# SwiGLU of a hybrid encoder block on one core: ten gate/up pairs become five token-major quads

## The chip, the core and the metric

The kernel runs on one core of a Trainium2 chip. The metric is the device time of one launch in microseconds (us), and of several runs the median. Five engines work side by side, each through its own list of instructions in order: TensorE (PE, with the loading of its stationary operand shown as PEld), VectorE (DVE), ScalarE (ACT), GpSimd (POOL) and SyncE (SP). In this kernel SP issues most transfers, POOL the others.

## The reference, cut to what matters

```python
x = x + merged @ w_o                 # two token mixers before this, unchanged here
h2 = rmsnorm(x, g_ffn)
x = x + (silu(h2 @ w_ff_gate) * (h2 @ w_ff_up)) @ w_ff_down
return rmsnorm(x, g_final)
```

There are 512 tokens, a model width of 1024 and a hidden width of 2816. All is float32. The change lies wholly in the third line.

## The kernel before, in words

Every operand x is split into a rounded part, hi, in the type fp32r and the remainder lo = x - hi (`split`, lines 200 to 210: ScalarE casts, VectorE subtracts). A product is three matmuls: hi hi, hi lo, lo hi. The large products go by the Strassen-Winograd scheme with seven products of quarters instead of eight. The forms of the activations are called a11, a12, a22, s1 to s4, those of the weights b11, b21, t1 to t4, b22.

`PLAN` lists the weight units in the order of use. `take` hands out the next unit and prepares two more: SP loads quarters into ten `raw` buffers, four entries of the plan earlier; VectorE adds quarters for the t forms (line 301); ScalarE and VectorE split the result into one of five buffers `whi` and `wlo`. For a few quads (`SUMMED`) the sums of quarters are made in DRAM by POOL's accumulating transfers, and VectorE adds nothing.

A Tile scheduler lays the instructions of every engine into a fixed order when the kernel is built; a wait is a semaphore. So the order on an engine is not that of the code, and an instruction that waits holds up all behind it on its engine.

SwiGLU runs like this. The hidden columns are 11 pairs of 256 gate and 256 up columns. A pair's quad is feature-major: the weight is the stationary operand, 256 tokens move past it, and the result has hidden features on the partitions and tokens along the free axis (`prod`, line 383; 24 matmuls of 256 columns per product). That is the layout that the down product needs for its stationary operand, so `gated` (lines 1125 to 1157) applies silu and the product and writes the seven activation forms straight from there. After 3, 7 and 11 pairs (`FF_PARTS`) comes a down product over the pairs since then, token-major (`prod_tm`, line 427; 512 columns per matmul, tokens on the partitions). The first two results go to DRAM through POOL (`put_first`, `add_y`), the last is joined with them and normalised.

`pair` (line 1173) holds the products of a pair; `beside` names products of later pairs that are put between, so that PE has something to do while a pair's activations are made.

Of the kernel before, what the change touches and what calls it, by code (L numbers as in the profile page):

```python
# [41 lines left out]
FF_PARTS = ((0, 3), (3, 4), (7, 4))  # L42
# [11 lines left out]
WIDTH = {"w": 512, "x": 256, "a": 512, "o": 512, "f": 256, "d": 512}  # L54
# [4 lines left out]


FIRST_PRODUCTS = ((0, "b11"), (0, "b21"), (1, "b11"), (1, "b21"), (2, "b11"), (2, "b21"))


def beside(q):

    if q < 5:
        return None, ((q + 6) // 2, "b21" if q % 2 else "b11")
    return (q, "b21"), (q + 1, "b11") if q + 1 < NQ else None


def plan():
# [42 lines left out]
    def f(q, *names):  # L114
        for n in names:
            out.append(("q", ("f", q), n, 0, 4))

    for q, name in FIRST_PRODUCTS:
        f(q, name)
    for q0, n in FF_PARTS:  # L120
        for q in range(q0, q0 + n):
            between, behind = beside(q)
            f(q, "t1", "t2")
            if between:
                f(*between)
            f(q, "t3")
            if behind:
                f(*behind)
            f(q, "t4", "b22")
        units = [(name, u) for name in FORMS for u in range(0, n, 2)]  # L130
        if q0 + n == NQ:

            i = units.index(("b21", 2))
            units[i:i + 3] = units[i + 1:i + 3] + units[i:i + 1]
        for name, u in units:
            out.append(("q", ("d", q0), name, u, min(2, n - u)))
    return out
# [9 lines left out]
SUMMED = (("f", 0), ("f", 1), ("o",))  # L147


def parts(quad):  # L150
    return (0, 2) if quad == ("o",) else (0,)


def loads():
# [3 lines left out]
    for i, x in enumerate(PLAN):  # L158
        if x[0] == "q":
            _, quad, name, u, nk = x  # L160
            need = name if quad in SUMMED else NEEDS.get(name)
            if need:
                out.append((i, quad, need, u, nk * WIDTH[quad[0]]))
# [4 lines left out]
QUARTERS = [x for x in LOADS if x[2][0] == "b"]  # L168
# [3 lines left out]
def block_kernel(ctx: ExitStack, tc: tile.TileContext, xw0, xw, xT, xtok, wpack, wquad, cols, decs, rot, g_ffn, g_final, out):  # L172
# [90 lines left out]
    steps = {"quads": sums_of(SUMMED[:2]), "heads": sums_of(SUMMED[2:])}  # L263
# [850 lines left out]
    gates = {}  # L1114

    q_add, gate_of = FF_PARTS[1][0], [None]

    def act_tiles(names):
        hi, lo = bigtile(F32R), bigtile(F32R)
        for j, n in enumerate(names):  # L1120
            act[n] = tuple(t[:, 2 * j:2 * j + 2, :].rearrange("p a (b c) -> p (a b) c", c=256) for t in (hi, lo))
        return hi.rearrange("p (f a) (b c) -> p f (a b) c", f=2, c=256), \
            lo.rearrange("p (f a) (b c) -> p f (a b) c", f=2, c=256)

    def gated(q, th, g, u):

        q0, _ = part_of[q]
        i = q - q0  # L1130
        if not gates.get(q0):
            t = bigtile(F32R)
            gates[q0] = [act_tiles(("a11", "a12")), act_tiles(("s1", "s3")), act_tiles(("s2", "s4"))]
            act["a22"] = tuple(t[:, 2 * j:2 * j + 2, :].rearrange("p a (b c) -> p (a b) c", c=256)
                               for j in range(2))
# [3 lines left out]
        nc.vector.tensor_tensor(out=s, in0=u, in1=s, op=ALU.mult)  # L1139

        def both(j, t):
            split(t.rearrange("p (s t) -> p s t", s=2), *(x[:, :, i, :] for x in gates[q0][j]))
        E, O = slice(0, 256), slice(256, 512)
        if th == 1:
            split(s[:, O], *(x[:, i, :] for x in act["a22"]))
        else:
            both(0, s)
        gates[q, th] = s
        if (q, 1 - th) not in gates:
            return  # L1150
        x1, x2 = gates.pop((q, 0)), gates.pop((q, 1))
        v, w = t512(), t512()
        for o, a, b, op in ((v[:, E], x2[:, E], x2[:, O], ALU.subtract), (v[:, O], x1[:, E], x2[:, E], ALU.subtract),
                            (w[:, E], v[:, E], x1[:, E], ALU.subtract), (w[:, O], x1[:, O], w[:, E], ALU.add)):
            nc.vector.tensor_tensor(out=o, in0=a, in1=b, op=op)
        both(1, v)
        both(2, w)
# [3 lines left out]
    def first_tokens(q, name):  # L1161

        _, (w,) = take()
        ps = bank()
        if name == "b11":
            prod(w, XF[0, 0], ps, True)
            heads_of[q] = {"a": ps, "p1": snap(ps)}
        else:
            prod(w, XF[1, 0], ps, True)
            g = heads_of[q]["p1"]  # L1170
            nc.vector.tensor_tensor(out=g, in0=ps, in1=g, op=ALU.add)

    def pair(q):
        st = heads_of[q]
        a, d = st["a"], bank()
        between, behind = beside(q)
        _, (w,) = take()
        if between:
            prod(w, XF["s1"], d, True)
            _, (w,) = take()  # L1180
            prod(w, XF["s2"], a, False)
            u2 = snap(a)
            first_tokens(*between)
        else:
            _, (w2,) = take()
            prod(w2, XF["s2"], a, False)
            u2 = snap(a)
            prod(w, XF["s1"], d, True)
# [235 lines left out]
```

## Time and profile before

| what | value |
|---|---|
| median of 3 runs | 1022.72 us (1022.34 to 1023.39) |
| profiled execution, first to last instruction | 1021.7 us |
| PE busy | 1013.2 us, 99% |
| VectorE busy | 902.5 us, 88% |
| ScalarE busy | 548.4 us, 54% |
| POOL busy | 151.7 us, 15% |
| moved by DMA | 202.34 MB, mean 198 GB/s |

The profile gives no time of its own for the profiled execution beside its span; the median of the runs is 1.0 us above the span. A row of a group reads: line, engine, operation, output and input tiles with shapes, count, then busy time, the mean of one in ns, and the idle time of the engine ahead of them with what ended it. A mean is the length of one instruction; where neighbours overlap, the engine's busy time is less than the sum of lengths. In the chain of waits the merged rows give start, length and the number of instructions.

### The profile page before, as it was taken

The numbers are of one execution on the slowest core, as the hardware profiler recorded it, in microseconds if no ns is written. First come the engines' busy times: TensorE is split into PE (matmuls) and PEld (weight loads), VectorE is DVE, ScalarE is ACT, GpSimd is POOL, SyncE is SP. The second block draws the span as 40 slices with busy tenths as digits, with TensorE's granted clock in tenths as the row PEclk, the third lists the DMA queues.
The fourth block names the chain that finished last, engine by engine and source line by source line (L and its number), as shares of the span: only waits on it lengthen the run. The fifth ranks groups of instructions, "written<-read, shape, count | busy, mean of one in ns | idle before, by whom it ended". The sixth has DMA issues, their size and how long they took to land.

```text
span 1021.7 us, 14821 instructions
## 1 busy us (share of the span) xinstructions
PE 1013.2 (99%) x5586; PEld 883.2 (86%) x5586; DVE 902.5 (88%) x1161; ACT 548.4 (54%) x744; POOL 151.7 (15%) x238
## 2 busy tenths in 40 slices
PE   9999999999999999999999999999999999999997
PEld 7888888888888998888888888889998999899986
DVE  7878998979798888797989997999898999889996
ACT  7547665553655455343543325586654565556554
POOL 0030221222122003202122100020001410110011
PEclk9999999999999999999999999999999999999999
DMA  9525587695767657839597855484316562663523
GB/s 354 188 81 185 173 296 212 214 310 162 249 196 238 250 203 268 333 130 349 124 331 294 272 200 169 157 264 132 107 42 242 172 154 83 198 153 104 165 69 98
DMA packets 53992, 202.34 MB, mean 198 GB/s; under 512 B 7392, under 2 KB 7520, under 8 KB 49312
## 3 DMA queue, kind: packets, MB, share of 16 engines
q1 hardware_dynamic: 37600, 137.39, 39.0%
q0 software_dynamic: 16032, 63.71, 21.3%
q8 instruction: 44, 0.72, 0.3%
q10 hardware_dynamic: 288, 0.29, 0.1%
q14 instruction: 28, 0.23, 0.1%
HBM read 162.82 MB, written 57.41 MB: 216 GB/s over the span
## 4 chain that ended last, share of the span: by engine, by line
PE 98%; DVE 1%; ACT 0%; issue 0%; POOL 0%; POOLq 0%; ACTq 0%
PE bank L427 39%; PE bank L383 27%; PE bank L342 10%; PE bank L343 10%; PE bank L344 10%; PE bank L477 0%; PE bank L1053 0%; PE bank L998 0%; PE bank L662 0%; DVE raw L301 0%; DVE big L1296 0%; ACT whi L203 0%; DVE wlo L204 0%; POOL fin L1286 0%; POOL ac L1035 0%
## 5 line engine op out<-in xcount | busy, mean ns | idle before, releaser
L203 ACT CAST whi<-raw 128x1024 fp32r<-128x1024 f32 (+2 forms) x299 | 302.8, 1028 | 265.0 <-PE bank L427 67.1
L204 DVE TENSOR_TENSOR wlo<-raw,whi 128x1024 fp32r<-128x1024 f32 (+2 forms) x300 | 352.7, 1192 | 68.0 <-ACT whi L203 67.7
L383 PE MATMUL bank<-xform,whi 128*128 128x256 f32 x1424 | 258.2, 284 | 0.3 <-ACT whi L203 0.3
L383 PEld LDWEIGHTS bank<-xform,whi 128*128 128x128 f32 x1424 | 222.3, 192 | 2.0 <-ACT t L434 0.8
L383 PE MATMUL bank<-xform,wlo 128*128 128x256 f32 x712 | 200.7, 283 | 0.0
L427 PE MATMUL bank<-whi,big 128*128 128x512 f32 x596 | 187.0, 389 | 0.0
L427 PE MATMUL bank<-whi,xform 128*128 128x512 f32 x496 | 157.1, 390 | 0.0
L301 DVE TENSOR_TENSOR raw<-raw 128x1024 f32<-128x1024 f32 (+1 forms) x128 | 152.0, 1203 | 4.2 <-DMA raw<-wquad 3.3
L383 PEld LDWEIGHTS bank<-xform,wlo 128*128 128x128 f32 x712 | 136.4, 192 | 0.0
L427 PEld LDWEIGHTS bank<-whi,big 128*128 128x128 f32 x596 | 111.9, 188 | 23.8 <-ACT t L434 0.4
L427 PE MATMUL bank<-wlo,big 128*128 128x512 f32 x298 | 115.7, 389 | 0.0
L427 PEld LDWEIGHTS bank<-whi,xform 128*128 128x128 f32 x496 | 93.0, 188 | 19.7 <-DVE xform L204 0.6
L427 PE MATMUL bank<-wlo,xform 128*128 128x512 f32 x248 | 96.5, 389 | 0.0
L434 ACT COPY t<-bank 128x512 f32<-128x512 f32 x105 | 61.0, 587 | 56.3 <-PE bank L383 30.1
L342 PE MATMUL bank<-big,whi 128*128 128x512 f32 x220 | 85.7, 390 | 0.0
L344 PE MATMUL bank<-big,wlo 128*128 128x512 f32 x220 | 85.6, 389 | 0.0
L343 PE MATMUL bank<-big,whi 128*128 128x512 f32 x220 | 85.6, 389 | 0.0
L427 PEld LDWEIGHTS bank<-wlo,big 128*128 128x128 f32 x298 | 56.0, 188 | 11.4
L427 PEld LDWEIGHTS bank<-wlo,xform 128*128 128x128 f32 x248 | 46.6, 188 | 9.6
L342 PE MATMUL bank<-whi,big 128*128 128x512 f32 x128 | 49.8, 389 | 0.0
L343 PE MATMUL bank<-wlo,big 128*128 128x512 f32 x128 | 49.8, 389 | 0.0
L344 PE MATMUL bank<-whi,big 128*128 128x512 f32 x128 | 49.8, 389 | 0.0
(203 smaller groups left out, 1385.8 us busy)
## 6 DMA issues: line engine op xcount, KB each, us to landing
raw<-wquad SPq DMA_DIRECT2D x140, 512.0 KB, 4.7
raw<-wpack SPq DMA_DIRECT2D x42, 512.0 KB, 6.3
t_f<-wquad POOLq DMA_DIRECT2D x12, 512.0 KB, 8.0
z<-t POOLq DMA_DIRECT2D x24, 256.0 KB, 4.5
t_o<-wquad POOLq DMA_DIRECT2D x12, 512.0 KB, 6.7
zform<-z POOLq DMA_DIRECT2D x6, 1024.0 KB, 7.8
v<-t POOLq DMA_DIRECT2D x16, 256.0 KB, 5.7
sg<-t POOLq DMA_DIRECT2D x16, 256.0 KB, 4.8
```

Of the source, the lines that this page charges most:

```text
L203: first = (round or nc.scalar.copy)(hi, src)
L204: low_of[0] = nc.vector.tensor_tensor(out=lo, in0=src, in1=hi.bitcast(F32), op=ALU.subtract)
L301: nc.vector.tensor_tensor(out=t, in0=t, in1=raws[quad, more, u][:, 0:n], op=ALU.add)
L342: nc.tensor.matmul(ps, lh, rh, start=first, stop=False)
L343: nc.tensor.matmul(ps, lh, rl, start=False, stop=False)
L344: nc.tensor.matmul(ps, ll, rh, start=False, stop=last)
L383: nc.tensor.matmul(o, l[:, c], r[:, k], start=start and s == 0 and k == 0 and i == 0, stop=stop and k == 3 and i == 2, skip_group_check=True)
L427: nc.tensor.matmul(pss[tt], l, r[:, c], start=start and k == 0 and i == 0, stop=stop and k == n - 1 and i == 2, skip_group_check=True)
L434: nc.scalar.copy(t, ps)
```

## The change

Ten of the eleven pairs become five quads of 512 gate and 512 up columns (`"g"` in the plan), computed token-major with `prod_tm`: activations are now the stationary operand, 512 weight columns move, a product is 24 matmuls of 512 columns. The eleventh pair (`LONE`) stays feature-major, through `fm_quad`.

A token-major result has tokens on the partitions. The down product needs hidden features there. So `gated` makes silu and product as before and then turns 32x32 blocks on VectorE, two transposes of 128 x 256 elements for each of the four token blocks of a quad. When the quad is done, `scatter` writes the turned tiles to DRAM with four transfers of 256 KB and reads them back with two of 512 KB, all on SP, so that the features land on the right partitions. `act_forms_of` then makes the forms of a whole quad: one cast and remainder of 1024 elements for a11 and a12, and forms of 512 elements instead of 256.

In that layout the tokens come in a permuted order (32-row blocks), so the down results are written to and read from permuted rows (`rows`). The parts are now 4, 4 and 3 blocks of 256 hidden columns. Only the first quad is in `SUMMED`, as two units where there were two pairs. In the third and fifth quads the first two products run before a down part, so quarter b11 is loaded a second time for t1 (`AGAIN`). The lone pair's products stand between the fifth quad and the last down part in the code.

```diff
-FF_PARTS = ((0, 3), (3, 4), (7, 4))
+FF_PARTS = ((0, 4), (4, 4), (8, 3))
+LONE = NFB // 2 - 1
...
-SUMMED = (("f", 0), ("f", 1), ("o",))
+SUMMED = (("g", 0), ("o",))
+AGAIN = (("g", 2), ("g", 4))
...
+    def act_forms_of(q, n, x1, x2):
+        tiles, i = slot(q)
+        hi, lo = ({k: area(t[j], i, n, k) for k, t in tiles.items()} for j in range(2))
+        split(flat(x1), flat(hi["a"]), flat(lo["a"]))
+        split(pairs(x2, 1), pairs(hi["z"], 0), pairs(lo["z"], 0))
+        x = [pairs(t, e) for t in (x1, x2) for e in range(2)]
+        s1, s3, s2, s4 = (t512()[:, 0:256 * n].rearrange("p (b t) -> p b t", t=P) for _ in range(4))
+        for o, a, b, op in ((s1, x[2], x[3], ALU.subtract), (s3, x[0], x[2], ALU.subtract),
+                            (s2, s1, x[0], ALU.subtract), (s4, x[1], s2, ALU.add)):
+            nc.vector.tensor_tensor(out=o, in0=a, in1=b, op=op)
+        for k, e, t in (("v", 1, s1), ("v", 0, s3), ("w", 0, s2), ("w", 1, s4)):
+            split(t, pairs(hi[k], e), pairs(lo[k], e))
...
+    def gated(i, j, g, u):
         s = t512()
         gate_of[0] = s
         nc.scalar.activation(s, g, AF.Silu)
         nc.vector.tensor_tensor(out=s, in0=u, in1=s, op=ALU.mult)
+        if i not in turned:
+            turned[i] = [misctile(D, "turned").rearrange("p (q i j r) -> p q i j r", q=2, i=4, j=4) for _ in range(2)]
+        for h, t in enumerate(turned[i]):
+            nc.vector.transpose(t[:, :, :, j, :].rearrange("p q i r -> p i q r"),
+                                s.rearrange("p (i q c) -> p i q c", i=4, q=4)[:, :, 2 * h:2 * h + 2, :])
+
+    def scatter(i):
+        tiles, at = slot(2 * i)
+        d = dram.tile([P, 4, 512], F32, name=f"turned{i}")
+        for h, t in enumerate(turned[i]):
+            for q in range(2):
+                nc.sync.dma_start(d[64 * h + 32 * q:64 * h + 32 * q + 32].rearrange("c b f -> b c f"),
+                                  t[:, q].rearrange("p i j r -> p (i j r)"))
+        x = [area(tiles[k][1], at, 2, k).bitcast(F32) for k in "wv"]
+        for b, t in enumerate(x):
+            nc.sync.dma_start(flat(t), d[:, 2 * b:2 * b + 2].rearrange("p b f -> p (b f)"))
+        act_forms_of(2 * i, 2, *x)
...
+    def rest(i, last_first=False, middle=False):
...
+        prod_tm(4, of(XF[1, 1]), a, False, True)
+        for tt in range(2):
+            gated(i, 2 + tt, a[tt], u3[tt])
+        prod_tm(4, of(XF["s4"]), d, False, True)
+        for tt in range(2):
+            nc.vector.tensor_tensor(out=u2[tt], in0=d[tt], in1=u2[tt], op=ALU.subtract)
+            gated(i, tt, p1[tt], u2[tt])
+        scatter(i)
...
+    rest(0, last_first=True)
+    rest(1, middle=True)
+    first_a(2)
+    first_b(2)
+    down(4, put_first)
+    rest(2)
...
+    first_a(3)
+    rest(3, middle=True)
+    first_a(4)
+    first_b(4)
+    down(4, add_y)
+    rest(4)
+    lone()
```

Three places of the new order, with the change's own line numbers. First, VectorE at the end of the second quad, ahead of the first down part. `t_6559` and `t_6561` are its last two results; L1251 and L1193 finish them, L1197 turns them, L206 with `wlo` are weight splits, L303 sums of weight quarters, and row 668 is the remainder of the activations that came back from DRAM, L1161 their forms.

```order
L1251 TENSOR_TENSOR t_6559<-bank,t_6559 128x512
L1251 TENSOR_TENSOR t_6561<-bank,t_6561 128x512
L1193 TENSOR_TENSOR t_6730<-t_6559,t_6730 128x512
L1193 TENSOR_TENSOR t_6736<-t_6561,t_6736 128x512
L1197 STREAM_TRANSPOSE turned<-t_6730 128x4x2x32 x2
L1197 STREAM_TRANSPOSE turned<-t_6736 128x4x2x32 x2
L206 TENSOR_TENSOR wlo<-raw,whi 128x1024 x2
L303 TENSOR_TENSOR raw<-raw 128x1024 x3
L206 TENSOR_TENSOR wlo<-raw,whi 128x1024 x2
L303 TENSOR_TENSOR raw<-raw 128x1024
L206 TENSOR_TENSOR big<-big 128x1024
L1161 TENSOR_TENSOR t_6752<-big 128x512
```

The same place of a pair before, where the forms follow the product at once:

```order
L1139 TENSOR_TENSOR t_8076<-t_7909,t_8076 128x512
L301 TENSOR_TENSOR raw<-raw 128x1024
L204 TENSOR_TENSOR big<-t_8076,big 128x2x256
L1155 TENSOR_TENSOR t_8081<-t_8076,t_8040 128x256
L1155 TENSOR_TENSOR t_8082<-t_8081,t_8076 128x256
```

Between a quad's last product and its first form there are now four transposes and eight instructions on weights, where there was one; the forms of a whole quad stand in one block behind them.

Second, SP at the fifth quad. `turned_8308` is the DRAM tile, L1206 the writes, L1210 the reads, L288 loads of weights, L1312 the load of the final norm's gains.

```order
L1206 DMA turned_8308<-turned 4x32x512 x4
L288 DMA raw<-wquad 128x1024
L1312 DMA gf<-g_final 128x1024
L1210 DMA big<-turned_8308 128x1024 x2
L288 DMA raw<-wquad 128x512
```

Two loads stand between the writes and the reads.

Third, ScalarE at the same place. `big_8306` and `big_8304` are the activations read back, `whi_8506` the first weight unit of the last down part, and `bank_8342` the result of the lone pair's first product.

```order
L205 CAST whi_8473<-raw_8208 128x1024
L205 CAST whi_8506<-raw_8376 128x1024
L205 CAST big_8315<-big_8306 128x1024
L205 CAST big_8321<-big_8304 128x512
L205 CAST big_8317<-t512_8326 128x4x128
L205 CAST big_8317<-t512_8327 128x4x128
L205 CAST big_8319<-t512_8328 128x4x128
L436 COPY t512_8374<-bank_8342 128x512
```

The copy of the lone pair's first bank stands behind five casts of the fifth quad's activations. PE has in its order three products of the lone pair (72 matmuls), then the twelve matmuls of the first down unit, then the lone pair's next product.

More of the change, by code (lines that the diff above doesn't have):

```diff
@@ L115, in f, with d @@
         for n in names:
[L116 to L129, printed above, removed]
+            if q == LONE:
+                out.append(("q", ("f", q), n, 0, 4))
+            else:
+                for u in (0, 2):
+                    out.append(("q", ("g", q), n, u, 2))
+    def d(q0, n):
         units = [(name, u) for name in FORMS for u in range(0, n, 2)]
@@ L1113, in block_kernel @@
     act = {}
[L1114 to L1125, printed above, removed]
-        q0, _ = part_of[q]
[L1130 to L1135, printed above, removed]
+    slots = {}
```

198 lines of the change are left out of this document (106 added, 92 removed).

## The prediction

> **What bounds the kernel now.** I read the page's summary first, then the chain of waits, then busy time by stretch of the feed-forward stage, then the groups of instructions there, and last the waits and the transfers.
>
> ```profile
> span 1021.7 us, 14821 instructions
> PE 1013.2 (99%) x5586; PEld 883.2 (86%) x5586; DVE 902.5 (88%) x1161; ACT 548.4 (54%) x744; POOL 151.7 (15%) x238
> PE 98%; DVE 1%; ACT 0%; issue 0%; POOL 0%; POOLq 0%; ACTq 0%
> ```
>
> TensorE (PE) is busy for 99% of the span and carries 98% of the chain that ends last: only fewer or faster matmuls, or a new stall of PE, can change the time. The chain in order of time gives the rate of both kinds of product, because it merges matmuls that run without a gap:
>
> ```profile
> 787.53 73.91 PE bank L383 x612
> 899.55 71.99 PE bank L383 x600
> 979.09 31.09 PE bank L427 x137
> 73.07 152.49 PE bank L427 x672
> ```
>
> L383 is the feature-major product, 256 columns per matmul: (73.91 + 71.99) / (612 + 600) = 120.4 ns. L427 is the token-major one, 512 columns: 31.09 / 137 = 226.9 ns, and 152.49 / 672 gives the same. Two of the first do the work of one of the second, so 240.8 ns becomes 226.9 ns.
>
> Now the engine that must feed PE, by stretch of SwiGLU (PE, PEld, DVE, ACT, POOL busy, then clock and DMA):
>
> ```profile
> 782.00:862.00 80.00, 79.70 (x645) 78.57 (x644) 75.73 (x91) 46.20 (x62) 16.30 (x13) 1.00 0.57 162
> 862.00:900.00 38.00, 38.00 (x172) 31.57 (x171) 34.76 (x40) 20.53 (x26) 5.26 (x6) 1.00 0.58 151
> 688.00:1011.00 323.00, 322.56 (x2281) 303.35 (x2280) 298.13 (x361) 186.81 (x256) 32.02 (x35) 1.00 0.46 131
> ```
>
> Over the 323 us from the first gate product to the last down product PE stands still for 0.4 us, and VectorE (DVE) is busy for 298.1, or 92%; in the gate/up stretch 782 to 862 it is 95%. The clock is 1.00 throughout. VectorE is the second bound, 25 us away, and it is the engine to which the change adds work.
>
> **What the change takes from PE.** Ten pairs were 10 x 7 x 24 = 1680 matmuls at 120.4 ns = 202.2 us; five quads are 5 x 7 x 24 = 840 at 226.9 = 190.6 us. Gain: **11.6 us**. The down products and the lone pair keep their matmuls.
>
> **What it gives to VectorE.** The groups by shape in this stage, and the only 32x32 transposes of the kernel:
>
> ```profile
> L204 DVE TENSOR_TENSOR wlo<-raw,whi 128x1024 fp32r<-128x1024 f32 x109 | 131.4, 1220 | 19.0 <-ACT whi L203 18.9
> L301 DVE TENSOR_TENSOR raw<-raw 128x1024 f32<-128x1024 f32 x56 | 67.8, 1219 | 1.1 <-DMA raw<-wquad 0.8
> L204 DVE TENSOR_TENSOR big<-t,big 128x512 fp32r<-128x512 f32 x33 | 22.6, 684 | 0.0
> L1155 DVE TENSOR_TENSOR t<-t,t 128x256 f32<-128x256 f32 x33 | 13.0, 418 | 0.0
> L204 DVE TENSOR_TENSOR big<-t,big 128x256 fp32r<-128x256 f32 x11 | 4.6, 418 | 0.0
> L1155 DVE TENSOR_TENSOR t<-t 128x256 f32<-128x256 f32 x11 | 4.6, 416 | 0.0
> L218 DVE STREAM_TRANSPOSE big<-big 32x512 f32<-32x512 f32 x64 | 45.0, 703 | 1.7 <-ACT big L905 0.8
> ...
> 920.74 1.23 DVE L204 TENSOR_TENSOR wlo<-raw,whi 128x1024 fp32r<-128x1024 f32 x1
> 921.88 0.42 DVE L204 TENSOR_TENSOR big<-t,big 128x256 fp32r<-128x256 f32 x1
> 922.22 0.69 DVE L1139 TENSOR_TENSOR t<-t,t 128x512 f32<-128x512 f32 x1
> ...
> 924.29 0.69 DVE L204 TENSOR_TENSOR big<-t,big 128x512 fp32r<-128x512 f32 x1
> 924.90 0.42 DVE L1155 TENSOR_TENSOR t<-t,t 128x256 f32<-128x256 f32 x1
> 499.89 5.01 DVE L218 STREAM_TRANSPOSE big<-big 32x512 f32<-32x512 f32 x7
> ```
>
> By the starts, neighbours overlap: a 1024 costs 921.88 - 920.74 = 1.14 us of the engine, a 512 0.61, a 256 0.34. The seven transposes don't: 5.01 / 7 = 0.72 each. A new transpose is 128 partitions x 256 elements, which no row shows. By elements per partition it is half of the 512 of L218, as the 256 of L1155 is 0.42 against 0.68: 0.43 us. By 32x32 blocks it is 32 blocks against 16: 1.41 us. I take 0.43, the row with the same length per lane, and keep 1.41 as a rival.
>
> The Trainium skill ("VectorE: DVE Perf Modes", The three transpose paths) says that the transpose uses one 32x32 array per bank and gives a grid of independent blocks. By that the four groups of 32 partitions go at once, which is the 0.43; no run yet shows it, and with 1.41 the sum below would be 39 us higher.
>
> Sum: 40 transposes + 17.2; the differences for Strassen's forms, 44 of 256 x 0.34 = 15.0, become 20 of 512 and 4 of 256 = 13.6, - 1.4; the rounding remainders of the activations, 33 x 0.61 + 11 x 0.34 = 23.9, become 5 x (1.14 + 5 x 0.61) + 0.61 + 5 x 0.34 = 23.3, - 0.6; the lone pair's two products become eight of 128 elements (0.21 by the same steps), + 0.5. Together **+ 15.7 us**: 298.1 + 15.7 = 313.8 us of VectorE, against 322.6 - 11.6 = 311.0 us of PE. The order has turned: VectorE now needs more time than PE has. Weight splits, sums of quarters and evictions keep their number; ScalarE keeps its casts and has room (187 of 323).
>
> **Where that becomes a stall.** VectorE can be late by what it is ahead.
>
> ```profile
> ACT whi L203 <- PE bank L383: 31.0, 30, 3.1
> SPq L286 <- DVE wlo L204: 230.9, 56, 22.5
> L203 ACT CAST whi<-raw 128x1024 fp32r<-128x1024 f32 x106 | 109.9, 1048 | 81.0 <-PE bank L383 28.3 <-DVE raw L301 26.1 <-PE bank L427 14.0
> ```
>
> The cast waits 30 times until PE frees one of five weight buffers, so VectorE is as far ahead as they allow: four units of 24 x 120.4 ns = 2.9 us, less cast and remainder (1.05 + 1.22), some 9 us. SP's loads wait in their turn for VectorE's buffers, so the 2 MB that are loaded a second time are early anyway: nothing, and if that lead were gone, one load's landing. A quad with sums costs VectorE 14 x 1.14 + 8 x 1.14 + 14 x 0.61 + 8 x 0.43 + 1.14 + 5 x 0.61 = 41.3 us, PE 168 x 0.227 = 38.1; a down part of four blocks costs 22 x 1.14 + 6 x 0.61 = 28.7 against 38.1. So the lead melts by 3 us in a quad and grows again in a down part: alone that would fit into 9 us. What does not fit is the trip through DRAM, which is new. Its nearest rows (KB each, us from issue to landing):
>
> ```profile
> raw<-wquad SPq DMA_DIRECT2D x58, 512.0 KB, 4.0
> first_part<-t POOLq DMA_DIRECT2D x8, 256.0 KB, 5.3
> ydr<-first_part POOLq DMA_DIRECT2D x8, 256.0 KB, 8.4
> raw<-wquad SPq DMA_DIRECT2D x4, 256.0 KB, 2.6
> big<-ydr SPq DMA_DIRECT2D x2, 512.0 KB, 5.0
> ...
> ydr<-big SPq DMA_DIRECT2D x8, 256.0 KB, 4.2
> GB/s 354 188 81 185 173 296 212 214 310 162 249 196 238 250 203 268 333 130 349 124 331 294 272 200 169 157 264 132 107 42 242 172 154 83 198 153 104 165 69 98
> ```
>
> A write of 256 KB from SP lies between 2.6 and 8.4; I take 4.2, the one that SP issues into DRAM. A read of 512 KB lies between 2.6 and 5.0; I take 4.0, the most frequent.
>
> *Joins 1 and 2* (second quad to first down part, fourth quad to second). From the quad's last matmul: 0.61 for the second bank, two products 1.2, four transposes 1.7, write 4.2, read 4.0, cast 1.05, remainder 1.22 = 14.0 us. Cover: two products of the next quad and the first unit of the down product, (48 + 12) x 0.227 = 13.6. Late by 0.4. Then VectorE has the block of forms in front of the next weights (the first order fence ahead): nine of 512 and two evictions, 11 x 0.61 = 6.7, a split 1.14, three sums 3.4, a split 1.14 = 12.4, and PE wants that unit after four units, 10.9: late by 1.5 more; some forms follow one another at 0.72 instead of 0.61, + 1. About **3 us** each.
>
> *Join 3* (fifth quad to the last down part). The lone pair is meant as cover, but PE's order takes only three of its seven products, 72 x 0.1204 = 8.7 us, and then the first down unit, which needs the fifth quad's activations. VectorE after the last matmul: two of 512, a split, two pairs of transposes = 0.61 + 0.86 + 0.61 + 1.14 + 0.86 = 4.1; write 4.2; in front of the read two loads of 512 KB on SP's queue (the second fence), 1.5 us each at the page's best slice, 354 GB/s: 3.0; read 4.0; cast and remainder 2.3 = 17.6. Late by **8.9**. Behind it ScalarE's copy of the lone pair's first bank, which PE's next product needs, waits until the casts are through (the third fence): four of 512 and two casts, 3.6 against the down unit's 2.7, + 0.9; the next down unit's split is behind 9 + 4 of 512 and itself, 9.1 against 2.7 + 0.9 + 2.9, + 2.6; the lone pair's own activations come two such steps later, + 2. Together **14 us**. Even a trip of no length would leave the eight 1024s that VectorE has in front of the remainder: 4.1 + 9.1 + 1.2 - 8.7 = 5.7.
>
> The Trainium skill ("DMA: Bandwidth & Descriptors", Queues, rings and completion order) says that an engine consumes the descriptors of a ring in order. No row here shows it; by it the read waits behind the two loads, and without it the sum would be 3 us lower.
>
> Sum against the profiled execution: 1021.7 - 11.6 + 3 + 3 + 14 = 1030.1. The median of the runs, 1022.72, is 1.0 above that span: **1031 us**. By the lowest rows (2.6 + 2.6, no loads ahead) the joins are held by the eight 1024s that VectorE does in between anyway: 2.5 + 2.5 + 11, 1027. By the highest (8.4 + 5.0) each join is 5.2 longer: 1047. The forecast's own range is 1026 to 1047.
>
> **Rivals.** *A, PE stays the bound (faster).* The lead of 9 us swallows the joins too. For it: no stretch of the trace has PE waiting for weights, although VectorE's share there reaches 95%. Against it: the down product waits for activations, for which no buffer runs ahead. If the three joins cost 0 to 8 us the time is 1022.7 - 11.6 + 0 to 8 = 1011 to 1019; up to 11.6 it is not slower. *B, VectorE sets the pace everywhere.* At its densest share, 75.73 / 80 = 0.947, 313.8 us take 331.4 against 323: + 8.4, 1031 again, but with PE's gaps spread over all five quads and none at the DRAM trips. *C, the transposes go block by block.* 40 x (1.41 - 0.43) = 39 us on an engine with no room: 1070. Against it L218's row, where 0.703 for 512 elements is what any other 512 costs. *Slower, then, from one mechanism:* forecast and B both; they decide as soon as the stalls pass 11.6 us.
>
> **How the numbers follow.** Forecast 0.50, A 0.27, B 0.17, C 0.06. The time is the forecast's, 1031. The range reaches into A down to 1013 and to 1046 above; outside are A's lowest part, C and the forecast's top, under 2 in 10. 0.2% is 2 us, about what a measurement can tell here. Faster by more: A but for its upper edge, 0.25. Within: that edge, the forecast's and B's lowest, 0.08. Slower: the rest, 0.67.
>
> **What would show it.** In the profile after: token-major matmuls at 227 ns and 11.6 us less PE work; 40 transposes at 0.43; VectorE 16 us busier; PE idle at three places, after the second, fourth and fifth quads, the last the longest, in front of a down matmul and behind the cast and remainder of the activations that came from DRAM. Spread gaps behind weight remainders would be B. A PE share still at 99% would be A and would make the forecast wrong: then the joins were covered.

## The result, and the profile after

The changed kernel takes **1181.59 us** (median of 4 runs, 1180.58 to 1185.11). The kernel before, run with it, takes 1023.06 (1022.34 to 1024.34). The ratio is 1.156, with an interval of 1.154 to 1.158. Slower was right; the size was not: 1031 had been predicted, with 1046 as the upper end, and the loss of 158.5 us is some nineteen times the 8.3 forecast.

Of the experiments below, one (the last join and two queues) has a run of 1267.26 us, at a clock of 0.75, against 1040.60 to 1042.50 in its other three, and its median is that of the three. The kernel before, run beside each group of experiments, took 1022.9 to 1023.5 us, so their times can be compared.

The page of the changed kernel: span, engines, the granted clock by slices, the chain of waits, DMA packets and GpSimd's queue.

```profile
span 1180.0 us, 13209 instructions
PE 1028.1 (87%) x4746; PEld 853.4 (72%) x4746; DVE 914.9 (78%) x1179; ACT 549.1 (47%) x736; POOL 149.7 (13%) x238
PEclk9999999999999999999999999798996979776965
PE 64%; issue 21%; DMA 7%; DVE 4%; POOL 2%; ACT 1%; SPq 0%; POOLq 0%; DVEq 0%; ACTq 0%
DMA packets 66209, 214.87 MB, mean 182 GB/s; under 512 B 15264, under 2 KB 15392, under 8 KB 61536
q0 software_dynamic: 23712, 63.77, 19.0%
```

PE has 840 matmuls fewer (5586 before), as the change says, and yet is busy for 14.9 us longer, since the clock digits fall in the last third of the slices: the work is less and runs slower. A fifth of the chain is "issue", time in which an engine waits for nothing that the profile shows. GpSimd's queue moves the same 64 MB as before in 23712 packets; before, it was 16032. The packets that carry an accumulation have not become smaller: the trace has 128 of 2 KB for each, as before, and the 384 more for each new one have 8 bytes.

Where PE stands still (each row ends with its idle time and what ended it):

```profile
758.26 0.80 PE L429 MATMUL bank<-whi,xform 128*128 128x512 f32 x1 [12.43 <-ACT t L436]
799.22 0.79 PE L429 MATMUL bank<-whi,big 128*128 128x512 f32 x1 [8.62 <-ACT big L205]
900.59 0.80 PE L429 MATMUL bank<-whi,xform 128*128 128x512 f32 x1 [19.81 <-ACT t L436]
950.95 0.80 PE L429 MATMUL bank<-whi,big 128*128 128x512 f32 x1 [12.12 <-ACT big L205]
1059.54 0.80 PE L385 MATMUL bank<-xform,whi 128*128 128x256 f32 x2 [13.73 <-ACT whi L205]
1080.38 0.80 PE L429 MATMUL bank<-whi,big 128*128 128x512 f32 x1 [13.19 <-ACT big L205]
1137.76 0.76 PE L429 MATMUL bank<-whi,big 128*128 128x512 f32 x1 [13.63 <-DVE bank L1374]
1149.12 0.80 PE L429 MATMUL bank<-wlo,big 128*128 128x512 f32 x1 [8.04 <-DVE wlo L206]
```

The second, fourth and sixth are the three joins that were predicted. The first and third lie inside the second and the fourth quad, where nothing was predicted; the fifth lies in the lone pair, whose weights ScalarE casts late because it waited for accumulations before; the last two lie in the last down part, behind loads of y that GpSimd adds to a result. Between the fourth row and the fifth there are four more of 2 to 7 us, 17.5 together, all ended by L436, ScalarE's copies of banks.

What stands behind the later ones is GpSimd's list of instructions. Before, eight accumulations onto y take 6.8 us to issue (first row, kernel before). Now they go one by one (four rows, kernel after):

```profile
813.24 6.82 POOL L1208 DMA_DIRECT2D ydr<-first_part  x8
```

```profile
884.34 1.11 POOL L1262 DMA_DIRECT2D ydr<-first_part  x1 [14.21 <-issue]
893.03 1.12 POOL L1262 DMA_DIRECT2D ydr<-first_part  x1 [7.58 <-issue]
1018.19 1.11 POOL L1262 DMA_DIRECT2D ydr<-t  x1 [8.42 <-issue]
1027.92 1.10 POOL L1262 DMA_DIRECT2D ydr<-t  x1 [8.62 <-issue]
```

Each holds GpSimd for 8.7 us or more, mostly some 9.7, and 20 of them come between 868 and 1138 us: 16 onto y and, at the end, four that add y to a result. The waits of the other engines show who pays (total, times, longest):

```profile
ACT t L1192 <- DMA ydr<-t: 22.2, 3, 9.1
ACT t L436 <- DMA ydr<-t: 19.6, 3, 9.1
ACT big L205 <- DMA big<-turned: 65.4, 7, 18.2
```

The first two: ScalarE wants a buffer that an accumulation still reads, and behind ScalarE stands PE, for want of a free bank. The third is the trip through DRAM, also dearer than forecast, as the chain of waits shows for the write and the read of the first and of the last quad:

```profile
735.76 12.15 DMA turned<-turned
748.54 5.28 DMA big<-turned
1062.81 12.24 DMA turned<-turned
1075.12 4.13 DMA big<-turned
```

The write takes 12.2 us where 4.2 was taken and 8.4 was the upper bound. Its four transfers together have no more under way than one accumulation has: they are 512 packets of 2 KB, 0.097 us each, and for 9.4 of the 12.5 us from the first packet to the last exactly four are under way.

The whole can be added up in three terms: PE's busy time, its idle time up to its last matmul, and the tail from there to the end. They are worked out from the span, PE's busy time on the page and the end of the last matmul. "Cold" is the part of PE's busy time above 1001.6 = 1013.2 - 11.6, which the matmuls would take at the full clock.

| kernel | profiled span | PE busy (cold) | PE idle | tail |
|---|---|---|---|---|
| before | 1021.7 | 1013.2 | 2.4 | 6.1 |
| after | 1180.0 | 1028.1 (26.5) | 126.1 | 25.8 |
| rows of y follow one another | 1114.4 | 1012.8 (11.2) | 74.4 | 27.2 |
| turned tiles written as whole rows | 1155.3 | 1032.0 (30.4) | 97.4 | 25.9 |
| both | 1086.0 | 1017.1 (15.5) | 41.6 | 27.3 |
| and final writes split | 1075.0 | 1014.5 (12.9) | 42.2 | 18.3 |
| and forms later | 1058.7 | 1014.4 (12.8) | 26.0 | 18.3 |
| and lone pair first | 1055.9 | 1009.0 (7.4) | 28.2 | 18.7 |
| same without the trip | 1038.3 | 1005.3 (3.7) | 14.7 | 18.3 |
| and last join, two queues | 1038.8 | 1007.1 (5.5) | 17.3 | 14.4 |

### The profile page after: what moved, and what is told of

The parts are those of the page before. It is cut to its first block, busy times and chain, and to the rows that moved or that the text cites. A ratio compares the mean times of both kernels' runs of the same rounds, so it can differ in the third digit from the quotient of the medians.

```text
span 1180.0 us, 13209 instructions
## 1 busy us (share of the span) xinstructions
PE 1028.1 (87%) x4746; PEld 853.4 (72%) x4746; DVE 914.9 (78%) x1179; ACT 549.1 (47%) x736; POOL 149.7 (13%) x238
## 3 DMA queue, kind: packets, MB, share of 16 engines
q0 software_dynamic: 23712, 63.77, 19.0%
## 4 chain that ended last, share of the span: by engine, by line
PE 64%; issue 21%; DMA 7%; DVE 4%; POOL 2%; ACT 1%; SPq 0%; POOLq 0%; DVEq 0%; ACTq 0%
PE bank L429 31%; PE bank L345 9%; PE bank L344 9%; PE bank L346 9%; PE bank L385 5%; DMA turned<-turned 3%; DMA ydr<-t 2%; DVE wlo L206 1%; POOL ydr L1262 1%; DMA big<-turned 1%; DMA big<-ydr 1%; DVE raw L303 1%; DVE t L1193 0%; ACT big L205 0%; DVE turned L1197 0%
## 5 line engine op out<-in xcount | busy, mean ns | idle before, releaser
L205 ACT CAST whi<-raw 128x1024 fp32r<-128x1024 f32 (+2 forms) x299 | 302.9, 1028 | 281.5 <-PE bank L429 96.5
L206 DVE TENSOR_TENSOR wlo<-raw,whi 128x1024 fp32r<-128x1024 f32 (+2 forms) x300 | 352.3, 1191 | 86.0 <-ACT whi L205 85.4
L429 PE MATMUL bank<-whi,xform 128*128 128x512 f32 x1056 | 338.8, 398 | 49.7 <-ACT t L436 49.7
L429 PEld LDWEIGHTS bank<-whi,xform 128*128 128x128 f32 x1056 | 202.3, 192 | 95.7 <-ACT t L436 52.5
L429 PE MATMUL bank<-whi,big 128*128 128x512 f32 x596 | 197.2, 406 | 50.4 <-ACT big L205 34.4
L429 PE MATMUL bank<-wlo,xform 128*128 128x512 f32 x528 | 209.0, 396 | 0.0
L429 PEld LDWEIGHTS bank<-whi,big 128*128 128x128 f32 x596 | 116.6, 197 | 79.3 <-ACT big L205 35.9
L303 DVE TENSOR_TENSOR raw<-raw 128x1024 f32<-128x1024 f32 (+1 forms) x128 | 151.4, 1203 | 0.8
L429 PEld LDWEIGHTS bank<-wlo,xform 128*128 128x128 f32 x528 | 101.5, 192 | 21.1
L436 ACT COPY t<-bank 128x512 f32<-128x512 f32 x105 | 60.7, 587 | 74.8 <-PE bank L429 41.8
L385 PE MATMUL bank<-xform,whi 128*128 128x256 f32 x304 | 57.5, 290 | 13.8 <-ACT whi L205 13.7
L206 DVE TENSOR_TENSOR big<-big 128x1024 fp32r<-128x1024 f32 (+1 forms) x22 | 23.8, 1098 | 56.4 <-ACT big L205 56.4
L385 PEld LDWEIGHTS bank<-xform,whi 128*128 128x128 f32 x304 | 49.0, 198 | 15.0 <-ACT whi L205 13.9
L205 ACT CAST big<-big 128x1024 fp32r<-128x1024 f32 (+1 forms) x22 | 20.9, 950 | 66.3 <-DMA big<-turned 65.4
L344 PE MATMUL bank<-whi,big 128*128 128x512 f32 x128 | 49.8, 389 | 0.0
L346 PE MATMUL bank<-whi,big 128*128 128x512 f32 x128 | 49.8, 389 | 0.0
```

Of the source, the lines that this page charges most:

```text
L205: first = (round or nc.scalar.copy)(hi, src)
L206: low_of[0] = nc.vector.tensor_tensor(out=lo, in0=src, in1=hi.bitcast(F32), op=ALU.subtract)
L303: nc.vector.tensor_tensor(out=t, in0=t, in1=raws[quad, more, u][:, 0:n], op=ALU.add)
L344: nc.tensor.matmul(ps, lh, rh, start=first, stop=False)
L346: nc.tensor.matmul(ps, ll, rh, start=False, stop=last)
L385: nc.tensor.matmul(o, l[:, c], r[:, k], start=start and s == 0 and k == 0 and i == 0, stop=stop and k == 3 and i == 2, skip_group_check=True)
```

## The experiments

Two theories stood at the start. T1: the pattern of 4 x 32 rows makes every accumulation of GpSimd slow, and what queues behind it blocks PE. T2: the trip at the joins is the loss, and the accumulations only wait along with it.

### Rows of y that follow one another

```diff
-        nc.sync.dma_start(ydr[nb * P:(nb + 1) * P, half * 512:(half + 1) * 512], yt)
+        nc.sync.dma_start(ydr.rearrange("(b j r) d -> j b r d", j=4, b=4)[nb][:, :, half * 512:(half + 1) * 512], yt)
...
     def rows(nb, half, of=yrows):
+        if of is yrows:
+            return ydr[nb * P:(nb + 1) * P, half * 512:(half + 1) * 512]
```

> The changed kernel, but the running sum of y in DRAM keeps its rows in the order in which the tiles have them: SyncE's first write of it (off PE's path) spreads the rows, and all 28 accumulations and loads of GpSimd and SyncE behind it take 128 rows that follow one another instead of 4 x 32. T1 (the accumulations onto 4 x 32 rows keep GpSimd's queue busy for 9.7 us each, and everything that waits behind them blocks PE): GpSimd issues them again 1 to 1.7 us apart, landing falls from 9.4 us to 8.4 or less, what is left of the loss is the three joins with a 12 us write; time 1060 to 1090. T2 (the trip through DRAM at the joins is the loss, the accumulations only wait along with it): at least 1165.

Measured: 1116.81 us, ratio 1.092 (1.090 to 1.093), 64.8 us less than the change. GpSimd issues the eight again without a pause:

```profile
868.47 6.82 POOL L1264 DMA_DIRECT2D ydr<-first_part  x8
905.34 0.79 PE L429 MATMUL bank<-whi,xform 128*128 128x512 f32 x1 [25.02 <-ACT t L436]
```

T2 falls. The four waits of 2 to 7 us, the one in the lone pair and the two in the last down part are gone as well. T1 has the cause of the larger part, but its 1060 to 1090 was too low: what remains is not the forecast's three joins alone but also waits inside the quads, the longest of 25 us (second row).

### The trip with whole rows

```diff
-        d = dram.tile([P, 4, 512], F32, name=f"turned{i}")
+        d = dram.tile([4, P, 512], F32, name=f"turned{i}")
...
-                nc.sync.dma_start(d[64 * h + 32 * q:64 * h + 32 * q + 32].rearrange("c b f -> b c f"),
-                                  t[:, q].rearrange("p i j r -> p (i j r)"))
+                nc.sync.dma_start(d[2 * h + q], t[:, q].rearrange("p i j r -> p (i j r)"))
...
-            nc.sync.dma_start(flat(t), d[:, 2 * b:2 * b + 2].rearrange("p b f -> p (b f)"))
+            for g in range(4):
+                src = d[g].rearrange("(b c) f -> c b f", b=4)[:, 2 * b:2 * b + 2]
+                nc.sync.dma_start(flat(t)[32 * g:32 * g + 32].rearrange("c (b f) -> c b f", b=2), src)
```

> The changed kernel, but the turned tiles go to DRAM as four writes of 128 rows that follow one another (instead of 4 x 32 each), and come back as eight reads of 32 partitions instead of two of 128. T1: the writes land in 4 to 5 us instead of 12.2, each of the three joins is some 5 to 7 us shorter, the accumulations stay 9.7 us apart; time 1155 to 1170. T2: the joins carry the loss; time 1120 or less.

Measured: 1156.52 us, ratio 1.131 (1.129 to 1.132), 25.1 us less than the change, as T1 said. The trip's bytes are the same; only the patterns differ.

### Both

The two diffs together.

> Both edits: rows of y that follow one another, and turned tiles written as 128 rows that follow one another. T1: what is left are the three joins as the prediction had them (3 + 3 + 14 us against 11.6 us less of PE); time 1028 to 1050, and a granted clock of TensorE near 1.00 again. T2: as the run with the fast trip alone, within 10 us.

Measured: 1087.66 us, ratio 1.063 (1.061 to 1.064). The gains add up (64.8 + 25.1 = 89.9, measured 93.9), so these are two separate costs. But 1028 to 1050 was missed by 38 us, so T1 as it stood was not the whole. PE's waits that are left:

```profile
753.58 0.79 PE L429 MATMUL bank<-whi,xform 128*128 128x512 f32 x1 [6.79 <-ACT t L436]
795.85 0.80 PE L429 MATMUL bank<-whi,big 128*128 128x512 f32 x1 [4.25 <-ACT big L205]
882.80 0.79 PE L429 MATMUL bank<-whi,xform 128*128 128x512 f32 x1 [11.46 <-ACT t L436]
930.78 0.79 PE L429 MATMUL bank<-whi,big 128*128 128x512 f32 x1 [4.25 <-ACT big L205]
```

and, by stretches (length, busy of PE, PEld, DVE, ACT, POOL, then clock and DMA), the ten microseconds behind the third of them:

```profile
883.00:888.00 5.00, 5.00 (x12) 3.92 (x13) 2.77 (x5) 0.75 (x2) 0.00 (x0) 0.51 0.31 127
888.00:893.00 5.00, 5.00 (x23) 4.12 (x22) 1.68 (x2) 3.17 (x4) 0.00 (x0) 1.00 0.28 86
```

Twelve matmuls in the first 5 us, 23 in the next: after a long wait PE runs at half speed for some 5 us. So this wait costs its length and about 2.5 us more. The tail is still 27.3 us.

### The pattern alone, in the kernel before

```diff
-        nc.gpsimd.dma_start(out=ydr[nb * P:(nb + 1) * P, half * 512:(half + 1) * 512], in_=t, accum_op=ALU.add)
+        nc.gpsimd.dma_start(out=rows(nb, half), in_=t, accum_op=ALU.add)   # 4 x 32 rows
```

The write of y and its later loads go to the same rows.

> The kernel before, with one thing of the change alone: the running sum of y in DRAM is written, accumulated on and loaded in 4 x 32 rows, as the change does it, and nothing else is touched (no quads, no transposes, no trip). T1: GpSimd's accumulations are 9 to 10 us apart, and the time rises by most of what the change lost behind its last down parts; 1060 to 1110. T2: nothing but a longer landing, 1023 to 1030.

Measured: 1093.52 us, ratio 1.070 (1.068 to 1.071). With no quad, no transpose and no trip, the pattern costs 70.4 us. PE's longest wait has 39 us, and in that time:

```profile
946.72 1.10 POOL L1212 DMA_DIRECT2D ydr<-t  x1 [8.60 <-issue]
977.68 0.58 PE L383 MATMUL bank<-xform,whi 128*128 128x256 f32 x1 [39.20 <-ACT t L434]
945.00:965.00 20.00, 0.00 (x0) 0.00 (x0) 1.70 (x4) 3.95 (x6) 2.22 (x2) 0.50 0.21 28
948.50:955.50 7.00, 0.00 (x0) 0.00 (x0) 0.00 (x0) 0.00 (x0) 0.00 (x0) 0.50 0.29 37
```

The last two rows (stretches, as above) say it: no transfers but accumulations run, and the DMA share is 0.21 with the pauses between them and 0.29 within one, where four or five of the 128 packets are under way for 6.5 of 7.3 us. The packets themselves take 0.24 us, against 0.22 in the kernel before, where mostly 15 to 18 are under way. The Trainium skill ("DMA: Bandwidth & Descriptors", Why a DMA increments its semaphore by 16 and not by 1) has the rule: a transfer is carried by the largest number of engines up to 16 that divides the slowest dimension of both patterns. By that, 4 x 32 x 512 goes to four engines; the four or five packets at a time agree.

### The same rows in four transfers

```diff
-        nc.gpsimd.dma_start(out=rows(nb, half), in_=t, accum_op=ALU.add)
+        for g in range(4):
+            nc.gpsimd.dma_start(out=rows(nb, half)[g], in_=t[32 * g:32 * g + 32], accum_op=ALU.add)
```

> The kernel before with the running sum of y in 4 x 32 rows (1093.5 us with one transfer for the 4 x 32), each accumulation and load of GpSimd made as four transfers of 32 rows. The rows lie in the same places; only the pattern of one transfer changes. T1b (a transfer whose outermost dimension is 4 long is spread over 4 of the 16 engines, which are then full for 9 us): the transfers of 32 rows spread over all 16, time 1023 to 1040. Rival T1c (accumulating on rows in four separate pieces is slow as such, however it is issued): 1080 or more.

Measured: 1023.53 us, ratio 1.0005 (0.9996 to 1.0015): all of the 70 us are back. The rows lie where they lay in the run above, and the loads of y that GpSimd adds are split likewise; each transfer is a quarter as large, and its outermost dimension is 32, not 4.

```profile
814.31 25.55 POOL L1213 DMA_DIRECT2D ydr<-first_part  x32
880.00:915.00 35.00, 35.00 (x213) 31.45 (x213) 29.19 (x29) 16.08 (x20) 25.43 (x32) 1.00 0.92 224
```

Four transfers of 32 rows take GpSimd 3.2 us where one of 4 x 32 held it for 9.7, and PE is busy throughout. Scattered rows as such cost nothing. What stays open is why GpSimd waits for one accumulation before it issues the next (room for descriptors, or the engines themselves). Twice the memory for descriptors, 4096 bytes, could have told; but then 39.3 KB per partition are left for the weight buffers, which need 40, so there is no time for such a kernel.

### The final writes

```diff
-            q.dma_start(rows(nb, j, outrows), t)
+            for g in range(4):
+                q.dma_start(outrows[nb][g][:, j * 512:(j + 1) * 512], t[32 * g:32 * g + 32])
```

> The changed kernel with rows of y and turned tiles that follow one another (1087.7 us), and the eight final writes of y, 4 x 32 rows each, split into four writes of 32 rows. T4 (those writes are the third place where 4 x 32 rows cost: 27 us from the last matmul to the end against 11.5 before): 1070 to 1078. Rival T5 (the end is late only because PE came late and cold): 1084 to 1090.

Measured: 1077.89 us, ratio 1.054 (1.052 to 1.055), 9.8 less than both repairs without it. The tail shrinks from 27.3 to 18.3 us, so the pattern cost time in a third place. (The kernel before has a tail of 6.1 us, not the 11.5 of the expectation.) Each of SyncE's seven final writes of 256 KB ends with four packets of 4 bytes after the change where it ended with 16 before, 28 against 112 in the trace, which again fits four engines. Of the 12 us that the tail is still longer than before, a second queue takes off some 4 (below); the rest has no run of its own. SyncE's rows of the final writes (before, then after):

```profile
1011.59 6.71 SPq L1300 DMA_DIRECT2D y<-big  x7
```

```profile
1152.83 15.56 SPq L1352 DMA_DIRECT2D y<-big  x7
```

### The forms later on ScalarE

In the run with both repairs the 6.8 and 11.5 us are ended by L436, ScalarE's copies. Its list shows why: the casts L205 of what comes back from DRAM, and of the forms made from it, stand ahead of the copies that free PE's banks. New theory T6: a trip that no matmul waits for yet still stops PE, through ScalarE's order.

```diff
-        scatter(i)
+        d = scatter(i)                  # the writes; gather: the reads and forms
+        if i in (0, 2):
+            late.append((i, d))
+        else:
+            gather(i, d)
...
         u3 = [snap(x) for x in a]
+        if late:
+            with tc.issue_after(snapped[0].ins):
+                gather(*late.pop())
```

> The run with the split final writes, and the activation forms of the first and the third quad (cast, remainder, Strassen's differences of what comes back from DRAM) ordered on ScalarE behind the next quad's copies of its banks. T6 (ScalarE's queue, in which the cast of the returned data stands in front of the copies that free PE's banks, makes PE wait 6.8 us in the second quad and 11.5 us in the fourth, each followed by some 8 us at half the clock): both gaps go, 20 to 27 us less than the run with the split final writes, 1045 to 1055. Rival T7 (VectorE has no room, the work only moves behind): within 8 us of that run.

Measured: 1059.02 us, ratio 1.035 (1.034 to 1.037), 18.9 less. Both waits are gone, PE's idle time falls from 42.2 to 26.0; the gain misses its lower bound of 20 by one, and the time its upper bound by 4. T7 falls. (After those waits the clock was low for some 5 us, not the 8 of the expectation.)

### More cover at the joins

```diff
+        ahead = [("b11", 0), ("t1", 0), ("b21", 0)]
+        units = ahead + [x for x in units if x not in ahead]
...
+    with tc.issue_after(mm_last[0].ins):          # the lone pair's last matmul
         prod_tm(n, forms["a11"], a, True, part=(0,))
+        prod_tm(n, forms["s1"], d, True, part=(0,))
+        prod_tm(n, forms["a12"], b, True, part=(0,))
```

> The run with the later forms, and more of PE's work between a trip and the first matmul that needs it: the down products begin with the first half of three products instead of one (8.2 us of PE instead of 2.7), and the last down part begins behind all seven products of the lone pair instead of behind three. T8 (what is left are the waits at the three joins, 4 to 5 us each, the last one more, with a cold clock behind each): 1015 to 1032. Rival B (VectorE, with 313.8 us of work against 311.0, now sets the pace): 1033 to 1045 with gaps spread over all quads.

Measured: 1057.4 us, ratio 1.034 (1.032 to 1.035); a miss for both theories. At the first two joins the edit did not do what it says: PE had already run the first halves of two products, and in the new order the third product's first half came behind the second halves of these two, so the cover did not grow. At the last join all seven lone products do come first, and the wait moves into them, 11.0 us in one piece, ended by L442, the same kind of copy as in T6. The first join, PE and then VectorE:

```profile
781.62 0.73 PE L433 MATMUL bank<-whi,big 128*128 128x512 f32 x2 [1.65 <-DVE big L208]
788.02 0.80 PE L433 MATMUL bank<-whi,big 128*128 128x512 f32 x1 [4.29 <-ACT big L207]
```

```profile
773.41 3.49 DVE L208 TENSOR_TENSOR wlo<-raw,whi 128x1024 fp32r<-128x1024 f32 x3
776.82 3.61 DVE L305 TENSOR_TENSOR raw<-raw 128x1024 f32<-128x1024 f32 x3
780.35 1.22 DVE L208 TENSOR_TENSOR big<-big 128x1024 fp32r<-128x1024 f32 x1
```

The data are back and cast by 776.2 (ScalarE's cast starts at 775.17 and takes 1.04); the remainder starts at 780.35, since VectorE has weights to do first.

### Fewer sums on VectorE

```diff
-SUMMED = (("g", 0), ("o",))
+SUMMED = (("g", 0), ("o",), ("g", 3))
```

GpSimd issues the sums behind its last instruction of the norm.

> The run with the covered joins (1057.4 us), and the fourth quad's weight sums (14 additions of 1024 columns, 14 x 1.15 = 16 us of VectorE) made by GpSimd's accumulating transfers instead, in the first quads' time. It frees VectorE in front of the second join alone; the first join stays as it was. T9 (VectorE, late with sums and remainders, holds the activations at the joins): the second join's two gaps (1.7 and 4.3 us) and the cold clock behind them go, the first join's stay; 8 to 12 us less, 1045 to 1050. Rival T10 (the trip through DRAM itself holds the activations): both joins keep their gaps, 1055 to 1060.

Measured: 1077.38 us, ratio 1.053 (1.051 to 1.055), 20.0 more than without, and outside both ranges. The quad has 8 such sums, not the 14 of the expectation; VectorE's busy time falls by 8.3 us. The second join's waits stay, 1.68 and 4.28, just like the first one's. And the sums' transfers take the bandwidth from the weights:

```profile
710.00:720.00 10.00, 4.35 (x16) 2.75 (x14) 0.00 (x0) 2.96 (x4) 1.61 (x2) 0.76 0.99 347
728.16 1.22 DVE L305 TENSOR_TENSOR raw<-raw 128x1024 f32<-128x1024 f32 x1 [19.81 <-DMA raw<-wquad]
```

At 347 GB/s VectorE waits 19.8 us for a load, and PE stands still twice in the first quad, for 5.5 and 10.8 us. What VectorE saves in a quad does not reach the join, which fits, without showing it, the prediction's view that its lead is held to the few weight buffers.

### Without the trip

```diff
-                nc.sync.dma_start(d[2 * h + q], t[:, q].rearrange("p i j r -> p (i j r)"))
...
+        x = [t.rearrange("p q i j r -> p (q i j r)").rearrange("p (b q e t) -> p b q e t", b=2, q=2, e=2)
+             for t in turned[i]]
```

> The run with the covered joins, without the trip: the activation forms are made straight from the transposed tiles, no write to DRAM and no read back (so the down products get activations whose 32-row blocks lie in the wrong places). T9 (VectorE): the joins keep most of their gaps, 1050 to 1057. T10 (the trip): the gaps at all three joins go, 1030 to 1042.

This kernel leaves out the move across partitions, so the down products take their features from the wrong partitions and its result is wrong; it serves for the time alone. Measured: 1041.32 us, ratio 1.017 (1.016 to 1.019): the trip, even repaired, is worth 16.1 us, within reach of T10's 1030 to 1042 and not of T9's. But T10's picture is not right either: the last join's 14 us fall to 2.9, while each of the first two keeps 4.6 of its 5.9, now behind another instruction:

```profile
776.21 0.79 PE L433 MATMUL bank<-wlo,xform 128*128 128x512 f32 x1 [4.64 <-DVE wlo L208]
```

That is a weight's remainder: the forms are early and the weights late. VectorE has no pause around the first join in either run (28.4 of 28.5 us busy with the trip, 24.1 of 24.2 without). So at the first two joins VectorE is the limit whichever it does first (T9), and at the last one the trip is (T10), though through ScalarE's order, as the next run shows.

### The last join and two queues for the end

```diff
-                q.dma_start(outrows[nb][g][:, j * 512:(j + 1) * 512], t[32 * g:32 * g + 32])
+                (nc.scalar if q is nc.sync and g > 1 else q).dma_start(
+                    outrows[nb][g][:, j * 512:(j + 1) * 512], t[32 * g:32 * g + 32])
...
-        if i in (0, 2):
+        if i in (0, 2, 4):
...
         u3 = snap(a)
+        if behind:
+            with tc.issue_after(snapped[0].ins):
+                behind()               # the fifth quad's forms
```

> The run with the covered joins (1057.4 us), with two things more: the activation forms of the fifth quad stand on ScalarE behind the lone pair's copies of its banks, and the final writes of 32 rows are shared by SyncE's and ScalarE's queues (28 of them took SyncE 15.5 us, about 0.55 each). T6 (a cast that waits for the trip, in front of the copies that free PE's banks): the 11.0 us gap in the lone pair goes, with its cold clock, and the end comes 5 to 7 us sooner; 1036 to 1046. Rival T9 (VectorE has to do the fifth quad's and the lone pair's forms in any case): the gap comes back in front of the down products; 1047 to 1054.

Measured: 1040.61 us, ratio 1.017 (1.015 to 1.019), 16.8 less, in the middle of what T6 said. The 11.0 us are gone; 1.5 are left in the lone pair, and the tail is 14.4.

### Remainders of the forms on GpSimd

```diff
-            split(t, pairs(hi[k], e), pairs(lo[k], e))
+            split(t, pairs(hi[k], e), pairs(lo[k], e), low=nc.gpsimd)
```

> The same, and the four remainders of Strassen's activation forms in each quad (512 columns, 0.61 us each on VectorE) made on GpSimd, which is idle there. T9 (at the joins VectorE's forms and weight remainders together are what PE waits for; without the trip PE waited 4.6 us for weight remainders): 2 to 3 us less at each of the first two joins, 3 to 8 us in all. Rival T11 (GpSimd is slower for each, or takes VectorE's time, and PE waits for its result): the same or more by up to 10 us.

Measured: 1065.3 us, ratio 1.041 (1.039 to 1.042), 24.7 more; T11, and by more than it said.

```profile
L208 POOL TENSOR_TENSOR big<-t,big 128x512 fp32r<-128x512 f32 x20 | 34.1, 1732 | 198.2 <-ACT big L207 110.8 <-DMA raw<-wquad 87.4
L1176 DVE TENSOR_TENSOR t<-big,t 128x512 f32<-128x512 f32 x5 | 8.2, 1645 | 1.7 <-POOL big L208 1.7
```

A remainder of 512 takes 1.73 us there against 0.68 on VectorE, and both first joins grow: the first waits 4.8, 4.3, 0.5 and 1.3 us where it was 1.7 and 4.3. VectorE is slowed as well: an instruction on the forms that runs beside these remainders (second row) takes it 1.65 us, against 0.69 in the run before, and its busy time rises by 4.2 us with 24 instructions fewer. So the latency of the forms counts at a join, not only VectorE's load.

No kernel of this study beats the kernel before. The best with a right result, 1040.61, has by the table PE's work less by 11.6 us, and against it 14.9 more idle time (11.9 of it at the first two joins), 5.5 cold and 8.3 of tail.

## Why the prediction was wrong, step by step

**What bounds the kernel** and **PE's gain of 11.6 us**: right. 1680 matmuls became 840, and a run of them in the chain of the changed kernel goes at the rate that was used, 27.38 / 120 = 228 ns:

```profile
691.27 27.38 PE bank L429 x120
L1197 DVE STREAM_TRANSPOSE turned<-t 128x256 f32<-128x256 f32 x40 | 14.9, 417 | 0.1
```

**The transposes at 0.43 us**: right, 417 ns, 14.9 us for the forty (second row); rival C is out. So the Trainium skill's 32x32 array per bank ("VectorE: DVE Perf Modes", The three transpose paths), cited then, agrees with the trace here. **VectorE + 15.7 us**: 914.9 against 902.5 is + 12.4. Near enough.

**VectorE as the second bound**: right that it is the limit at the first two joins, shown by the run without the trip. Rival B, pace set everywhere, is out: between the joins PE has no wait of 0.5 us or more once the forms are moved. Rival A, joins covered, is out as well.

**The trip through DRAM**: the mechanism was right, the size wrong. The write was priced by a row of 128 rows in a line (4.2, bounds 2.6 to 8.4), and the changed kernel's write has 4 x 32 rows: 12.2. Bounds from the nearest rows do not hold where the new transfer has another pattern; with the waits that it brings inside the quads, 25.1 us in all. With the pattern repaired and the forms moved, the three joins wait 5.3, 5.4 and 13.1 us (the run with the later forms); 3, 3 and 14 were predicted. That sum, 24 against 20, was near, but at the first two joins the order was the other way round: VectorE does weights first, and 4.3 of the 5.3 us are a wait for a form, where the prediction had a wait for weights behind the forms. These joins alone cost more than PE's 11.6 us, so that the change was slower is not luck.

**"The joins are three"**: wrong. Trips 1 and 3 were given no price because no matmul needs their data soon. Yet their casts stand in ScalarE's order ahead of the copies that PE's banks wait for: 6.8 and 11.5 us with the trip repaired, 12.4 and 19.8 in the change; 18.9 us by the run that moved them. The prediction named what is queued behind the wait at the last join, and did not ask the same behind the first and third quads.

**The step that failed most is one that is not there.** The change's permuted rows got no term in the sum. They cost 64.8 us at the accumulations and 9.8 at the final writes. The prediction counted every transfer that was new and passed over those that were only rewritten; the diff shows them in one line, `rows`. The page of the kernel before had only the price of rows in a line (6.2 to 8.4 us to landing, issued without a pause), and nothing in it could show the other; the rule of the Trainium skill, cited above, would have.

**The clock** was taken as 1.00 because no stretch had less. It is 1.00 because PE never waits. Each long wait brought some 3 to 6 us at half speed, and the matmuls took 26.5 us more over the run. The Trainium skill ("TensorE: Matmul & The Clock Gate", Part 1) says that an idle window of about 3.4 us halves the clock and that about as much busy time restores it; for the fall the rows agree: 4.29 us of idle time does it, 1.65 doesn't. The way back took 3.0 to 6.4 us here, from the end of such a wait.

**The 2 MB loaded twice** at no cost: nothing in the traces speaks against it; it was not measured by itself.

## What to carry to other kernels

When a layout is permuted, price every transfer that touches it anew, also those whose bytes, place and time in the program stay the same: here one transfer of 4 x 32 rows held its queue three times as long as four transfers of 32 rows. Where new data arrive late, look along each in-order engine for what stands behind their first consumer, not only for the matmul that needs them. And a kernel at full clock has no reserve for a stall: add about half of the cold stretch, here 2.5 us, to each wait of some 4 us or more.

## What the runs showed that was not expected

An accumulation of 256 KB in a 4 x 32 pattern has four or five packets under way at a time (DMA share 0.29) and lands after 9.4 us, and GpSimd does not issue past it. SyncE's final writes to 4 x 32 rows are held up too: from the first to the last of seven issues 15.6 us against 6.7. Split into 28 they took SyncE 15.5 us as well, but landed sooner, and only a second queue brought that down, to 9.6 us for 14.
